# PEER's one-hot grids: which side of the matmul carries the weight, and a contiguous copy of the other side

## The chip, the cores and the metric

The kernel runs on one core of a Trainium2 chip. The metric is the device time of one execution in microseconds (us). Before the change it is 3071.65 us, the median of three runs (3069.44 to 3080.57).

## The reference

Two transformer blocks run one after the other on 512 tokens of width 1024. The change lies in the last layer of the second block, PEER: each token picks 128 of 16384 one-neuron experts (8 heads, 16 each), by two indices i and j of 128 each.

```python
def one_chunk(hb):
    q = (hb @ w_q).reshape(C, PEER_HEADS, 2, PEER_DK_HALF)
    s = jnp.einsum('thpd,hpnd->thpn', q, sub_keys)
    sv, si = lax.top_k(s, PEER_TOPK)
    ...
    fv, fpos = lax.top_k(cand, PEER_TOPK)
    eidx = jnp.take_along_axis(cidx, fpos, axis=-1).reshape(C, PEER_HEADS * PEER_TOPK)   # i * 128 + j
    g = jax.nn.softmax(fv, axis=-1).reshape(C, PEER_HEADS * PEER_TOPK)
    u = u_tab[eidx]
    a = jax.nn.gelu(jnp.einsum('ted,td->te', u, hb), approximate=False)
    coef = (g * a).astype(hb.dtype)
    return jnp.einsum('te,ted->td', coef, v_tab[eidx])
```

## The kernel before

The first 128 tokens take their rows of the tables `u` and `v` by gather (`own`, L1293): an indirect DMA on GpSimd (POOL) for each of 256 rows and one VectorE instruction on each (L1309 or L1313). The other 384 tokens are computed dense. For every j, `act` (L1267) loads a block of 128 experts, splits it into a high and a low part (`whi` by ScalarE L102, `wlo` by VectorE or POOL L103), multiplies it with all 384 tokens in 24 matmuls of 384 columns (L122 to L124) and writes the GELU (L1274). These products must then be multiplied by each token's gates, and for that each token gets a grid of 128 x 128 numbers, zero but at its 128 experts.

A grid is one small matrix product over the token's 128 picks. The picks lie on the 128 partitions. On one side stands a one-hot row of i for each pick, on the other a one-hot row of j times the pick's gate. The gate is held as two f16 parts (`WW[:, 0]` and `WW[:, 1]`), so a grid is two matmuls that add into the same place in PSUM, of 128 columns each, and both load the same stationary one-hot anew.

VectorE makes the one-hots for four tokens at a time (`onehots`, L1442; `OT` is 4), in a layout in which the token is the innermost index: element (i, token) of a tile lies at 4 i + token, so that the 128 values of one token are 8 bytes apart in f16. A set is four VectorE instructions: `oi` by comparing with i (L1450), `on` by comparing with j (L1452), and `on` times each of the two gate parts into `oj` (L1455, twice). `oi` and `oj` have three buffers (`OB`), `on` two.

`grids` (L1458) takes 128 tokens in 32 units of four tokens; a unit is eight matmuls (L1475, four tokens by two gate parts) into one PSUM bank, and a ScalarE instruction that moves the bank to the tile `G` (L1477). There are three such groups of tokens, so 96 units and 768 of these matmuls. Between the units the program sets other work: `unit` (L1497) adds .6508 expert blocks and .7 gathered rows to each unit of the first two groups, .7484 and .8 in the third; the picking of the next group of tokens (`picks`) runs in between. A scheduler turns this program into one order for each engine; each engine then works through its own order and waits where a semaphore is not up yet.

Of the kernel before, what the change touches and what calls it, by code (L numbers as in the profile page):

```python
# [11 lines left out]
F16 = mybir.dt.float16  # L12
# [4 lines left out]
OP = mybir.AluOpType  # L17
# [14 lines left out]
OT, OB, HL = 4, 3, 4  # L32
# [8 lines left out]
class Kern:  # L41
# [1198 lines left out]
    def peer(self):  # L1240
        nc, tc, I = self.nc, self.tc, self.I
        mm = nc.tensor.matmul
# [6 lines left out]
        with ExitStack() as cx:  # L1249
# [7 lines left out]
            IT, JT = [pi.tile([128, TD], F16, name=n) for n in ("IT", "JT")]  # L1257
            WW = pi.tile([128, 2, TD], F16, name="WW")
# [71 lines left out]
            for h in range(2):  # L1330
                bk = self.bank("x")
# [23 lines left out]
            with tc.tile_pool(name="pe2", bufs=2) as q2:  # L1355
# [4 lines left out]
                for hp in range(16):  # L1360
                    bk = bks[hp] if hp < 3 else self.feat_major(wq(hp), hT)
                    qT = q2.tile([128, T], F32, name="qT")
                    nc.scalar.copy(qT, bk)
                    bk = self.bank("x")
# [77 lines left out]
            def onehots(t, done):  # L1442
                sh = [128, OT // 4, 128, 4]
                of = lambda v: v.rearrange("p (g t) -> p g t", t=4)[:, :, None, :].to_broadcast(sh)
                io = io4[:, None].to_broadcast(sh)
                for tk in range(t * 128 - 128, t * 128, OT):
                    oi, on = [q4.tile(sh, F16, name=n, bufs=b) for n, b in (("oi", OB), ("on", 2))]
                    oj = q4.tile([128, 2] + sh[1:], F16, name="oj", bufs=OB)
                    done.append((oi, oj))
                    nc.vector.tensor_tensor(oi, io, of(IT[:, tk:tk + OT]), op=OP.is_equal)  # L1450
                    yield
                    nc.vector.tensor_tensor(on, io, of(JT[:, tk:tk + OT]), op=OP.is_equal)  # L1452
                    yield
                    for w in range(2):
                        nc.vector.tensor_mul(oj[:, w], on, of(WW[:, w, tk:tk + OT]))  # L1455
                        yield

            def grids(t):  # L1458

                gout = iter(())  # L1460
                hots = []
                hot = onehots(t, hots)
                for _ in range(HL):
                    next(hot)
                for c in range(128 // CT):
                    G = gp.tile([128, 128, CT], F32, name="G")
                    for u in range(0, CT, 4):
                        bk = self.bank("x")
                        for _ in range(16 // OT):
                            next(hot, None)  # L1470
                        if u % OT == 0:
                            oi, oj = hots.pop(0)
                        for e in range(4):
                            for w in range(2):
                                mm(bk[:, e * 128:(e + 1) * 128], oi[:, u % OT // 4, :, e], oj[:, w, u % OT // 4, :, e],  # L1475
                                   start=(w == 0), stop=(w == 1))
                        nc.scalar.activation(G[:, :, u:u + 4], bk.rearrange("p (t j) -> p j t", t=4), AF.Copy,  # L1477
                                             scale=1.0 / WSC)
                        if u % 8 == 4:
                            next(gout, None)  # L1480
                        yield
                    n = (t - 1) * (128 // CT) + c
                    gout = spill(n, G)
                    if n >= CD - KG:
                        last.append(G)
                        gout = iter(())
                for _ in gout:
                    pass

            def spill(c, G):  # L1490
                for k in range(0, 128, 2048 // CT // 2):
                    n = 2048 // CT // 2
                    nc.sync.dma_start(gd[c, 0:128, k * CT:(k + n) * CT], G[:, k:k + n].rearrange("p j t -> p (j t)"))
                    yield
# [19 lines left out]
            for t in range(NT):  # L1514
                if t == 0:
                    for _ in picks(t):
                        pace(FA, 0)
                    for u in range(1, NT):
                        for _ in tops(u):
                            pace(FT, S0)  # L1520
                    cs.close()
                    q4 = cy.enter_context(tc.tile_pool(name="pe3b", bufs=2))
                    gp = cx.enter_context(tc.tile_pool(name="pegg", bufs=2, side="right"))
                    prev = iter(())
                    continue
                for _ in picks(t):
                    pace(FB, S1)
                    unit(prev, 3)
                unit(prev, 128)
                late[0] = t - 1  # L1530
                prev = grids(t)
# [155 lines left out]
```

## Time and profile before

| | |
|---|---|
| time, median of three runs | 3071.65 us |
| time of the profiled execution | 3062.43 us |
| its span, first to last instruction | 3060.7 us |
| busy TensorE (PE), VectorE (DVE), ScalarE (ACT), POOL | 2933.6, 2093.2, 1156.9, 636.3 us |
| mean granted TensorE clock | 0.980 |
| the grids: first and last matmul of L1475 start at | 2000.2 and 2387.0 us |

The profile is of one execution. Times in it are counted from the first instruction. PE is the matmuls, PEld the loading of the stationary operand, which runs beside them. A matmul's record reaches to the end of its passage through the array, so that neighbours' records overlap: how fast matmuls follow each other is read from their starts, not from their durations. "Idle before, releaser" says what an engine waited for.

### The profile page before, as it was taken

How to read it: one execution, taken by the hardware profiler on the slowest of the kernel's cores; microseconds unless marked ns; L12 is line 12 of the kernel's file. 1: busy time of each engine (PE TensorE's matmuls, PEld its weight loads, DVE VectorE, ACT ScalarE, POOL GpSimd, SP SyncE). 2: the span in 40 equal slices, each digit the busy share in tenths (PEclk: the TensorE clock that was granted, in tenths of full speed). 3: DMA queues.
4: the chain of work that ended last, by engine and by line, in shares of the span. 5: the costliest groups of instructions: out<-in, count | busy, mean ns of one | idle time of the engine just before them, and what ended most of it. 6: DMA issues, size and time to landing. Idle time of an engine off the chain costs nothing.

```text
span 3060.7 us, 43629 instructions
## 1 busy us (share of the span) xinstructions
PE 2933.6 (96%) x16121; PEld 2473.6 (81%) x16121; DVE 2093.2 (68%) x4710; ACT 1156.9 (38%) x1918; POOL 636.3 (21%) x593
## 2 busy tenths in 40 slices
PE   7987998999999999999999999999999999999998
PEld 6765887888888788888865888889999888787887
DVE  7773767333255666425775778999988488787887
ACT  5634333322233322223565433343443333333332
POOL 1033220000000000000000004435444334444443
PEclk9988999999999999999999999999999999999999
DMA  4356553223343277432220225678888899999996
GB/s 141 96 144 184 148 146 127 91 96 96 90 131 103 83 237 231 138 95 89 85 70 8 88 96 192 223 251 305 288 292 284 276 327 336 315 329 324 323 329 228
DMA packets 217555, 569.04 MB, mean 186 GB/s; under 512 B 64475, under 2 KB 80091, under 8 KB 217213
## 3 DMA queue, kind: packets, MB, share of 16 engines
q1 hardware_dynamic: 144508, 362.71, 36.4%
q0 software_dynamic: 64096, 200.89, 19.4%
q10 hardware_dynamic: 8736, 2.65, 0.4%
q8 instruction: 126, 2.06, 0.3%
q14 instruction: 89, 0.72, 0.1%
HBM read 504.24 MB, written 61.87 MB: 185 GB/s over the span
## 4 chain that ended last, share of the span: by engine, by line
PE 74%; DVE 12%; DMA 7%; issue 4%; ACT 2%; POOL 1%; POOLq 0%; DVEq 0%; ACTq 0%; SPq 0%
PE b L276 18%; PE b L124 15%; PE b L123 15%; PE b L122 15%; DMA gl<-ga 3%; PE b L1475 3%; DVE wlo L103 2%; DVE hr L1313 1%; DVE er L1309 1%; PE b L1166 1%; DMA er<-in_pe_ur,eu 1%; PE b L964 1%; DVE wk L1344 1%; DMA sp_v<-vv 1%; PE b L1184 1%
## 5 line engine op out<-in xcount | busy, mean ns | idle before, releaser
L102 ACT CAST whi<-wst 128x1024 fp32r<-128x1024 f32 (+2 forms) x491 | 510.4, 1041 | 1162.1 <-PE b L123 483.3
L103 DVE TENSOR_TENSOR wlo<-wst,whi 128x1024 fp32r<-128x1024 f32 (+2 forms) x466 | 563.5, 1211 | 442.2 <-ACT whi L102 420.0
L124 PE MATMUL b<-hTh,wlo 128*128 128x384 f32 (+2 forms) x1992 | 718.0, 361 | 14.9 <-DVE wlo L103 14.7
L122 PE MATMUL b<-hTh,whi 128*128 128x384 f32 (+2 forms) x1992 | 723.3, 364 | 2.9 <-ACT hTh L223 1.9
L123 PE MATMUL b<-hTl,whi 128*128 128x384 f32 (+2 forms) x1992 | 718.2, 361 | 2.1 <-DVE hTl L224 2.1
L124 PEld LDWEIGHTS b<-hTh,wlo 128*128 128x128 f32 x1992 | 379.0, 190 | 58.2 <-DVE wlo L103 19.5
L122 PEld LDWEIGHTS b<-hTh,whi 128*128 128x128 f32 x1992 | 380.5, 191 | 42.8 <-ACT hTh L223 2.6
L123 PEld LDWEIGHTS b<-hTl,whi 128*128 128x128 f32 x1992 | 379.6, 191 | 40.9 <-DVE hTl L224 2.9
L122 PE MATMUL b<-whi,ch 128*128 128x512 f32 x768 | 304.9, 397 | 5.9 <-ACT ch L102 5.9
L123 PE MATMUL b<-wlo,ch 128*128 128x512 f32 x768 | 304.9, 397 | 2.4 <-DVE wlo L103 2.4
L124 PE MATMUL b<-whi,cl 128*128 128x512 f32 x768 | 304.9, 397 | 1.2 <-DVE cl L103 1.2
L1297 POOL DMA_INDIRECT er<-in_pe_v,ev x128 | 191.2, 1494 | 251.5 <-DVE hr L1313 227.5
L1297 POOL DMA_INDIRECT er<-in_pe_ur,eu x128 | 167.0, 1305 | 89.7 <-DVE er L1309 57.7
L122 PEld LDWEIGHTS b<-whi,ch 128*128 128x128 f32 x768 | 144.9, 189 | 40.4 <-ACT ch L102 6.2
L123 PEld LDWEIGHTS b<-wlo,ch 128*128 128x128 f32 x768 | 144.9, 189 | 37.8 <-DVE wlo L103 3.6
L124 PEld LDWEIGHTS b<-whi,cl 128*128 128x128 f32 x768 | 144.8, 189 | 36.7 <-DVE cl L103 1.9
L1313 DVE SCALAR_TENSOR_TENSOR hr<-er,a,hr 128x1024 f32<-128x1024 f32 x127 | 166.5, 1311 | 0.1
L1309 DVE SCALAR_TENSOR_TENSOR er<-er,hr 128x1024 f32<-128x1024 f32 x128 | 157.2, 1231 | 4.8 <-DMA er<-in_pe_ur,eu 4.7
L1279 POOL DMA_DIRECT2D ga<-gl x112 | 64.9, 579 | 347.6 <-ACT gl L1274 333.7
L276 PE MATMUL b<-whi,hTh 128*128 128x512 f32 (+2 forms) x336 | 129.3, 386 | 0.8 <-ACT P L976 0.8
L276 PE MATMUL b<-whi,hTl 128*128 128x512 f32 (+2 forms) x336 | 129.4, 385 | 0.4 <-DVE hTl L103 0.4
L276 PE MATMUL b<-wlo,hTh 128*128 128x512 f32 (+2 forms) x336 | 129.6, 386 | 0.0
(558 smaller groups left out, 4922.7 us busy)
## 6 DMA issues: line engine op xcount, KB each, us to landing
wst<-in_pe_u SPq DMA_DIRECT2D x128, 512.0 KB, 5.0
wst<-in_pe_v SPq DMA_DIRECT2D x128, 512.0 KB, 6.3
wst<-in_ffn_gu SPq DMA_DIRECT2D x88, 512.0 KB, 3.7
wst<-in_ad_w SPq DMA_DIRECT2D x48, 512.0 KB, 4.1
wst<-in_ffn_dn SPq DMA_DIRECT2D x44, 512.0 KB, 3.6
ga<-gl POOLq DMA_DIRECT2D x112, 192.0 KB, 4.2
gl<-ga SPq DMA_DIRECT2D x112, 192.0 KB, 5.4
gd<-G SPq DMA_DIRECT2D x40, 512.0 KB, 6.8
```

The lines of the kernel that those rows point to most:

```text
L102: self.nc.scalar.copy(hi, src)
L103: (eng or self.nc.vector).tensor_sub(lo, src, hi)
L122: mm(out, a[0], b[0], start=start, stop=False)
L123: mm(out, a[0], b[1], start=False, stop=False)
L124: mm(out, a[1], b[0], start=False, stop=stop)
L276: self.nc.tensor.matmul(banks[t][:, :n], self.chunk(aT, a, k + kk)[:, t * 128:(t + 1) * 128], w[b][:, kk, :], start=seen[t] == 1, stop=see ...
L964: self.nc.tensor.transpose(bk[:, c * 128:(c + 1) * 128], src[:, c * 128:(c + 1) * 128], self.ident)
L1279: nc.gpsimd.dma_start(ga[j], act(j))
L1297: d = nc.gpsimd.indirect_dma_start(out=r, out_offset=None, in_=src, in_offset=bass.IndirectOffsetOnAxis(ap=idx[:, k:k + 1], axis=0))
L1309: d = nc.vector.scalar_tensor_tensor(r, r, 1.0, hr, op0=OP.mult, op1=OP.mult, accum_out=a0[:, k:k + 1])
L1313: d = nc.vector.scalar_tensor_tensor(y0, r, a0[:, k - 128:k - 127], y0, op0=OP.mult, op1=OP.add)
L1475: mm(bk[:, e * 128:(e + 1) * 128], oi[:, u % OT // 4, :, e], oj[:, w, u % OT // 4, :, e], start=(w == 0), stop=(w == 1))
```

## The change

The two gate parts go to the i side, which stays in the interleaved layout and stays the stationary operand; `oi` now has the two parts and `os` is the plain one-hot from which they are made. The j side is a plain one-hot, `on`, made first; ScalarE copies it into `oj` with each token's 128 values side by side, and that copy is the moving operand. A set is still four VectorE instructions, and one ScalarE instruction more. `oj` shrinks to half, `oi` doubles, and `os` (two buffers) is new.

```diff
-                    oi, on = [q4.tile(sh, F16, name=n, bufs=b) for n, b in (("oi", OB), ("on", 2))]
-                    oj = q4.tile([128, 2] + sh[1:], F16, name="oj", bufs=OB)
+                    os, on = [q4.tile(sh, F16, name=n) for n in ("os", "on")]
+                    oi = q4.tile([128, 2] + sh[1:], F16, name="oi", bufs=OB)
+                    oj = q4.tile([128, OT, 128], F16, name="oj", bufs=OB)
                     done.append((oi, oj))
-                    nc.vector.tensor_tensor(oi, io, of(IT[:, tk:tk + OT]), op=OP.is_equal)
+                    nc.vector.tensor_tensor(on, io, of(JT[:, tk:tk + OT]), op=OP.is_equal)
+                    nc.scalar.copy(oj, on.rearrange("p g i t -> p (g t) i"))
                     yield
-                    nc.vector.tensor_tensor(on, io, of(JT[:, tk:tk + OT]), op=OP.is_equal)
+                    nc.vector.tensor_tensor(os, io, of(IT[:, tk:tk + OT]), op=OP.is_equal)
                     yield
                     for w in range(2):
-                        nc.vector.tensor_mul(oj[:, w], on, of(WW[:, w, tk:tk + OT]))
+                        nc.vector.tensor_mul(oi[:, w], os, of(WW[:, w, tk:tk + OT]))
                         yield
...
                             for w in range(2):
-                                mm(bk[:, e * 128:(e + 1) * 128], oi[:, u % OT // 4, :, e], oj[:, w, u % OT // 4, :, e],
+                                mm(bk[:, e * 128:(e + 1) * 128], oi[:, w, u % OT // 4, :, e], oj[:, u % OT + e],
                                    start=(w == 0), stop=(w == 1))
```

Line numbers of the changed kernel are two higher behind the function: the grids' matmul is L1477 there and the move to `G` is L1479; the copy is L1452, the two comparisons are L1451 (`on`) and L1454 (`os`), the products L1457. The order of the matmuls on TensorE is nearly the same: runs of 24 matmuls of an expert block and then one or two units of grids.

ScalarE in the third group of tokens, before; `G` is the grid tile, `whi` the high part of an expert block, `gl` its GELU, and what an instruction waits for stands in brackets:

```order
L1477 ACTIVATE G<-b_21342 128x128x4 [waits PE_49]
L1477 ACTIVATE G<-b_21359 128x128x4 [waits PE_49]
L102 CAST whi<-wst 128x1024 [waits DMAHW0_49,DVE_49,PE_49]
L1274 ACTIVATE gl<-b_21383 128x384 [waits DMASW1_49,PE_49]
L1477 ACTIVATE G<-b_21415 128x128x4 [waits DMAHW2_49,DMAHW4_49,DMAHW1_49,PE_49]
L102 CAST whi<-wst 128x1024 [waits DMAHW1_49,DVE_49,PE_49]
L1274 ACTIVATE gl<-b_21438 128x384 [waits DMASW3_49,PE_49]
```

and the same place now:

```order
L1479 ACTIVATE G<-b_21516 128x128x4 [waits PE_49]
L1479 ACTIVATE G<-b_21535 128x128x4 [waits PE_49]
L1452 COPY oj<-on 128x512 [waits DVE_49] x2
L102 CAST whi<-wst 128x1024 [waits DMAHW0_49,PE_49]
L1274 ACTIVATE gl<-b_21561 128x384 [waits DMASW1_49,PE_49]
L1479 ACTIVATE G<-b_21593 128x128x4 [waits DMAHW2_49,DMAHW4_49,DMAHW1_49,PE_49]
L1452 COPY oj<-on 128x512 [waits DVE_49]
L102 CAST whi<-wst 128x1024 [waits DMAHW1_49,PE_49]
L1274 ACTIVATE gl<-b_21618 128x384 [waits DMASW3_49,PE_49]
```

Behind each move to `G` there is now a copy, which waits for VectorE, and the next `whi` stands behind it.

VectorE in the third group of tokens, before; `wlo` is the low part of an expert block, `er` a gathered row:

```order
L1452 TENSOR_TENSOR on<-io_14630,JT 128x512 [waits DVE_49]
L1450 TENSOR_TENSOR oi<-io_14630,IT 128x512 [waits PE_49]
L1455 TENSOR_TENSOR oj<-on,WW 128x512 x2
L103 TENSOR_TENSOR wlo<-wst,whi 128x1024 [waits DMAHW6_49,Activation_49]
L1309 SCALAR_TENSOR_TENSOR er,a_14638<-er,hr 128x1024 [waits DMASW2_49]
```

and now:

```order
L1451 TENSOR_TENSOR on<-io_14630,JT 128x512 [waits Activation_49]
L1454 TENSOR_TENSOR os<-io_14630,IT 128x512 [waits DVE_49]
L1457 TENSOR_TENSOR oi<-os,WW 128x512 [waits PE_49]
L1457 TENSOR_TENSOR oi<-os,WW 128x512
L1457 TENSOR_TENSOR oi<-os,WW 128x512 [waits DVE_49,PE_49]
L1457 TENSOR_TENSOR oi<-os,WW 128x512
L1309 SCALAR_TENSOR_TENSOR er,a_14638<-er,hr 128x1024 [waits DMASW4_49]
```

The wait for TensorE has moved from the comparison to the first product, and the comparison that makes `on` now waits for ScalarE, which must have copied the `on` of two sets before.

## Rows read from the trace of the kernel before

**Rows 1.** The page's first part: busy us (share of the span) xinstructions.

```profile
PE 2933.6 (96%) x16121; PEld 2473.6 (81%) x16121; DVE 2093.2 (68%) x4710; ACT 1156.9 (38%) x1918; POOL 636.3 (21%) x593
```

**Rows 2.** Stretches of the grids and after: us, busy by engine, clock, DMA share, GB/s.

```profile
2000.00:2260.00 260.00, 257.99 (x1628) 248.86 (x1628) 244.92 (x505) 112.22 (x172) 119.51 (x104) 0.99 0.82 283
2260.00:2390.00 130.00, 130.00 (x825) 125.48 (x825) 102.01 (x192) 51.01 (x81) 62.42 (x57) 1.00 0.84 287
...
2430.00:2700.00 270.00, 264.81 (x1155) 217.89 (x1156) 213.34 (x394) 92.31 (x128) 105.46 (x82) 0.98 0.92 319
```

**Rows 3.** Waits of DVE, 2000 to 2260, then 2260 to 2390: us, times, longest.

```profile
DVE oi L1450 <- PE b L1475: 6.1, 10, 2.3
DVE wlo L103 <- ACT whi L102: 5.6, 2, 2.8
DVE er L1309 <- DMA er<-in_pe_ur,eu: 1.9, 1, 1.9
...
DVE oi L1450 <- PE b L1475: 18.8, 19, 2.2
DVE wlo L103 <- PE b L1475: 5.8, 1, 5.8
DVE wlo L103 <- ACT whi L102: 1.9, 1, 1.9
```

**Rows 4.** Timeline of PE around two runs of grid matmuls: start us, us, what.

```profile
2154.53 1.11 PE L1475 MATMUL b<-oj,oi 128*128 128x128 f16 x8
2155.40 0.42 PE L122 MATMUL b<-hTh,whi 128*128 128x384 f32 x1
2155.66 0.34 PE L123 MATMUL b<-hTl,whi 128*128 128x384 f32 x1
...
2164.93 2.06 PE L1475 MATMUL b<-oj,oi 128*128 128x128 f16 x16
2166.74 0.43 PE L122 MATMUL b<-hTh,whi 128*128 128x384 f32 x1
2167.01 0.33 PE L123 MATMUL b<-hTl,whi 128*128 128x384 f32 x1
```

**Rows 5.** Timeline of PE, matmuls of 256 columns that lie side by side.

```profile
1743.25 0.28 PE L123 MATMUL b<-hTl,whi 128*128 128x256 f32 x1
1743.36 0.28 PE L124 MATMUL b<-hTh,wlo 128*128 128x256 f32 x1
...
1744.88 0.28 PE L122 MATMUL b<-hTh,whi 128*128 128x256 f32 x1
```

**Rows 6.** PEld by line and shape: busy us, mean ns of one | idle before.

```profile
L122 PEld LDWEIGHTS b<-hTh,whi 128*128 128x128 f32 x1992 | 380.5, 191 | 42.8 <-ACT hTh L223 2.6 <-ACT whi L102 1.1 <-ACT hTh L102 0.4
L1475 PEld LDWEIGHTS <-oi 128*128 128x128 f16 x768 | 81.3, 118 | 21.5 <-issue 15.7 <-DVE oj L1455 2.7 <-DVE on L1452 1.1
...
L778 PEld LDWEIGHTS b<-wlo,M 128*64 128x64 f32 x256 | 24.1, 138 | 0.9 <-issue 0.5 <-POOL wlo L768 0.3
```

**Rows 7.** Timelines cut inside the run at 2164.93: its first loads, its first matmuls.

```profile
2164.92 0.15 PEld L1475 LDWEIGHTS <-oi 128*128 128x128 f16 x2 [0.16 <-issue]
...
2164.93 0.29 PE L1475 MATMUL b<-oj,oi 128*128 128x128 f16 x1
...
2164.93 0.41 PE L1475 MATMUL b<-oj,oi 128*128 128x128 f16 x2
...
2164.93 0.53 PE L1475 MATMUL b<-oj,oi 128*128 128x128 f16 x3
```

**Rows 8.** Timeline of PE: small matmuls in close order.

```profile
308.28 0.92 PE L754 MATMUL b<-Nd,Y 128*64 128x64 f32 x24 [0.37 <-ACT Y L746]
```

**Rows 9.** ACT by line, 2000 to 2390: busy us, mean ns of one | idle before.

```profile
L102 ACT CAST whi<-wst 128x1024 fp32r<-128x1024 f32 x70 | 73.8, 1054 | 199.9 <-PE b L123 166.9 <-issue 32.0 <-ACT whi L102 1.0
L1477 ACT ACTIVATE G<-b 128x512 f32<-128x512 f32 x96 | 56.6, 593 | 17.3 <-PE b L1475 15.4
L1274 ACT ACTIVATE gl<-b 128x384 f32<-128x384 f32 x70 | 33.9, 484 | 0.0
```

**Rows 10.** DVE by line, 2000 to 2390: the one-hot instructions.

```profile
L1455 DVE TENSOR_TENSOR oj<-on,WW 128x512 f16<-128x512 f16 x192 | 100.2, 563 | 0.0
...
L1450 DVE TENSOR_TENSOR oi<-io,IT 128x512 f16<-128x512 f16 x94 | 39.3, 420 | 25.1 <-PE b L1475 24.9
L1452 DVE TENSOR_TENSOR on<-io,JT 128x512 f16<-128x512 f16 x95 | 38.2, 417 | 0.0
```

## The prediction

> **What bounds the kernel now.** I began with the busy shares of the page [rows 1]: TensorE is busy 96% of the span, VectorE 68%, so time comes from TensorE, if at all. Then the same by stretches [rows 2], since the change touches only 2000 to 2390 us: there TensorE is busy 388 of 390 us, and VectorE is close behind, 244.9 of 260 us while two groups of grids run beside the picking of the next group, then 102.0 of 130 us. VectorE's waits [rows 3] say who leads: for 6.1 us of the first stretch and 18.8 us of the second it waits for a buffer that the grid matmuls still read. So TensorE decides the stage, with a margin over VectorE of 15.1 us in the first stretch and 28.0 us in the second. What TensorE saves counts in full only up to these margins.
>
> **What a grid matmul costs.** Two timelines give it by a difference that has the same edges on both sides [rows 4]: from the start of a run of 8 to the second matmul behind it is 2155.66 - 2154.53 = 1.13 us, from a run of 16 it is 2167.01 - 2164.93 = 2.08 us. Eight more cost 0.95 us, 119 ns each. The 768 cost 91 us.
>
> What are those 119 ns? Matmuls of 256 columns that lie side by side follow each other in 116 ns (14 steps from 1743.25 to 1744.88) [rows 5], so a grid matmul of 128 columns takes as long as one of 256: half rate. It might be the load of the stationary side instead. A load's record is 191 ns for 128 columns of f32 and 138 ns for 64 [rows 6]: 53 ns per 64 columns on top of some 85 ns that are the same for both. The grids' f16 load is 118 ns, which leaves 33 ns of loading. The run's start agrees [rows 7]: the first two loads are over after 0.15 us, so the second ends some 0.03 us after the first; yet the ends of the first three matmuls lie 0.12 us apart (0.29, 0.41, 0.53). The second matmul had its stationary side in time and still came 0.12 us later. So I take it that the moving side is streamed at half rate, and that its step of 8 bytes is the reason: it is what sets it apart from the matmuls of [rows 5].
>
> **The change part by part.**
>
> *Moving side contiguous.* 128 columns at the rate of [rows 5] are 58 ns. Small matmuls with a load each follow at under 0.92 / 24 = 38 ns [rows 8], so the issue of a pair doesn't stand in the way, and 33 ns of load fit beside 58. No row shows f16 columns side by side: the bounds are 119 ns (the step is not the reason, nothing saved) and 58 ns. I take 60 ns, near the lower end, because of [rows 7]. Saved: 59 ns x 768 = 45 us of TensorE, 30 us of it in the first stretch (512 matmuls), 15 us in the second (256).
>
> The Trainium skill has a measured pace for this: TensorE: Matmul & The Clock Gate, section "Back-to-back issue gap", gives about 81 ns for each pair of load and matmul at 128 columns in a real kernel. No row here has such a pair. By it 38 ns x 768 = 29 us would be saved, 19 and 10 us in the two stretches.
>
> *Stationary side with two parts.* Still 768 loads, with the same 8-byte step: 118 ns each as before, beside the matmuls. Nothing.
>
> *VectorE.* Two comparisons and two products a set before and after, of the same size and layout [rows 10]: nothing, in work. The wait for a free buffer moves from the first instruction to the third, which is better by up to 0.8 us a set where VectorE waits for TensorE.
>
> *The copy on ScalarE.* 96 copies of 512 elements. There is no such row; the nearest are 593 ns for 512 elements out of PSUM in a scattered order, 484 ns for 384, 1054 ns for 1024 in order [rows 9]. I take 0.6 us (0.5 if the f16 source helps, 1.2 if the step of 8 bytes halves it): 58 us. ScalarE is busy 163 of 390 us [rows 2], so 221 with it. The copies stand in front of the next `whi`, and before that cast ScalarE has idled 166.9 us over 70 casts for TensorE to release its buffer [rows 9], 2.4 us each; one or two copies (0.6 to 1.2 us) fit into that. Cost nothing there; without that cover it would be 58 us on ScalarE's chain, and the expert blocks would come late.
>
> *The new wait.* `on` waits for the copy two sets back. Behind it VectorE holds the products that TensorE wants, and `wlo`. That copy stands behind the move to `G` of a unit some four sets back, which is earlier than the matmuls for which the first product waits anyway. Where all is on time it costs nothing; with 0.05 us of handshake on some 60 of the 96 sets I take 3 us, bounds 0 and 1.2 us (a move and a copy) on every set.
>
> *What ends last then.* In the first stretch TensorE would need 260 - 30 = 230 us, VectorE 244.9: VectorE takes over. Of its 15.1 us of waits the 6.1 us for TensorE go, and about half of the 5.6 us for a `whi` that itself waits for TensorE [rows 3]: 9 us gained. In the second stretch TensorE needs 115 us, VectorE 102: all 15 us are gained. 9 + 15 - 3 = 21 us. The stage becomes 6% shorter, so the DMA rate must rise from 287 to about 303 GB/s; later the kernel moves 319 [rows 2]. What follows the grids shifts forward as it is.
>
> The profiled execution took 3062.4 us (span 3060.7), and becomes 3041. The median of the runs is 9.2 us above it; I take the 21 us off that: 3051 us.
>
> **The rivals.**
>
> *The step costs nothing.* Then the 119 ns are something in the f16 load or its order, and stay. For it: the load's record, 118 ns [rows 6], is within 1 ns of the pace, as if each pair waited for its load, and no matmul here differs from the grids in the step alone. Against it: [rows 7]. TensorE saves nothing, VectorE and ScalarE stay covered: 0 to +4 us, 3072 us.
>
> The Trainium skill speaks for this one: SBUF — State Buffer, section "Specifications (TRN2)", says that memory lines have 16 bytes and that two hits in a line are enough for full bandwidth. A step of 8 bytes has just two. By that rule the moving side ran at full rate before; [rows 4] do not look like it, but do not exclude it.
>
> *The handshake decides (slower).* VectorE has 15.1 us of slack in the first stretch for 64 sets, so a wait of 0.24 us a set at `on` is the point from which it, and not TensorE, makes the stage longer. If ScalarE is held at a `whi` while a copy stands behind it, the wait is about one copy, 0.6 us: 64 x 0.6 - 15 = +23 us; in the second stretch 32 x 0.6 = 19 us against 28 - 15 = 13 us of slack, +6 us against the 15 us gained. 3072 + 23 + 6 - 15 = 3086 us. For it: the waits in the new order. Against it: the copy needed lies two sets back.
>
> *VectorE is no bound.* Its products average 563 ns where the comparisons take 417 to 420 [rows 10]; 192 x 0.14 = 28 us that the work itself, the same 512 elements, does not explain. If these go when TensorE runs ahead, the first stretch gains its 30 us too, and all 45 us come through: 3027 us.
>
> **How the numbers follow.** Forecast (pace 58 to 85 ns, VectorE takes over in the first stretch) 0.60, own range 3040 to 3062; step costs nothing 0.20; handshake 0.10; no bound by VectorE 0.10. About 0.5% (15 us) is what a measurement of this kernel can tell from no change: 3056 to 3087. Faster: 0.47 of the forecast's 0.60 and the last rival, 0.57. Slower: the worse part of the handshake and 0.02 of the second, 0.08. Same 0.35. The range 3032 to 3076 us leaves out the better part of the last rival (0.07), the handshake from its middle on (0.08) and a little of the first rival.
>
> **What would show it.** Right: eight more grid matmuls cost about 0.48 us; copies near 0.6 us; TensorE now waits for `oi` between 2000 and 2250, and not after; the grids end about 21 us sooner. Wrong: a pace still near 119 ns (the step was not it); VectorE idle at `on` L1451 for ScalarE by more than 15 us; `whi` late, so that TensorE waits in expert blocks; or a stage that gets shorter by 40 us.

## The result and the profile after

| | before | after |
|---|---|---|
| median (lowest to highest), 4 runs each | 3076.11 us (3069.44 to 3087.63) | 3046.45 us (3018.76 to 3054.05) |
| profiled execution, its span | 3062.43, 3060.7 us | 3054.05, 3051.4 us |
| first and last grid matmul | 2000.2, 2387.0 us | 2004.9, 2365.9 us |

The ratio is 0.9896, with a 95% interval of 0.9858 to 0.9935: about 1% faster. The profiled execution after is the slowest of its four, so its span shows less than the median does; the stage itself can be read in it all the same.

The page's first part, after, answers to [rows 1]:

```profile
PE 2906.6 (95%) x16121; PEld 2440.9 (80%) x16121; DVE 2090.9 (69%) x4710; ACT 1209.1 (40%) x2014; POOL 647.3 (21%) x593
```

TensorE is busy for 27 us less in this execution and ScalarE for 52 us more, in 96 instructions more; VectorE's work is the same. The three groups of 128 tokens, each from its first grid matmul to the next group's, first before and then after (columns as in [rows 2]: us, then busy of PE, PEld, DVE, ACT and POOL, clock, DMA share, GB/s):

```profile
2000.20:2131.30 131.10, 129.32 (x812) 124.29 (x811) 125.47 (x270) 55.37 (x85) 58.53 (x51) 0.99 0.79 277
2131.30:2263.10 131.80, 131.77 (x832) 127.40 (x832) 121.49 (x240) 58.21 (x89) 61.57 (x54) 1.00 0.84 289
2263.10:2387.00 123.90, 123.90 (x791) 119.65 (x791) 99.20 (x188) 48.88 (x77) 59.44 (x54) 1.00 0.83 286
```

```profile
2004.90:2132.80 127.90, 117.95 (x811) 113.08 (x812) 125.49 (x270) 72.41 (x118) 66.88 (x51) 0.95 0.82 291
2132.80:2256.40 123.60, 121.08 (x831) 116.24 (x832) 121.81 (x246) 75.53 (x122) 65.64 (x54) 0.97 0.85 296
2256.40:2365.90 109.50, 109.50 (x793) 105.95 (x792) 93.39 (x181) 64.20 (x106) 60.42 (x53) 1.00 0.91 324
```

In the third group TensorE was busy all the time and still is: its 14.4 us come through whole. In the first two VectorE has the same 247 us of work, and the groups have shrunk from 262.9 to 251.5 us, close to that. TensorE is now the one that waits, 10 us of it in the first group. Together the grids take 361.0 us instead of 386.8: 25.8 us.

Waits of PE from 1995 to 2400, first before and then after, then those of DVE after, from 2005 to 2256 and from 2256 to 2370 (us, times, longest), for [rows 3]:

```profile
PE b L1475 <- DVE oj L1455: 8.7, 2, 6.9
```

```profile
PE b L1477 <- DVE oi L1457: 17.2, 4, 7.1
PE b L124 <- DVE wlo L103: 2.0, 1, 2.0
```

```profile
DVE on L1451 <- ACT oj L1452: 1.9, 2, 1.2
...
DVE oi L1457 <- PE b L1477: 2.3, 3, 1.0
DVE on L1451 <- ACT oj L1452: 0.6, 1, 0.6
```

VectorE waits for TensorE for 2.3 us instead of 24.9, and none of it in the first two groups. For the copy it waits 2.5 us in all. Of TensorE's waits, 6.9 us before and 6.8 us after lie ahead of the first grid matmul, and so outside the groups. The longest wait of TensorE stands at the change from the first group to the second, where VectorE has the picking of tokens on its hands:

```profile
2132.80 0.30 PE L1477 MATMUL b<-oj,oi 128*128 128x128 f16 x1 [7.14 <-DVE oi L1457]
2132.86 0.67 PE L122 MATMUL b<-hTh,whi 128*128 128x384 f32 x1
2133.33 0.97 PE L1477 MATMUL b<-oj,oi 128*128 128x128 f16 x7
```

The matmul of 384 columns behind it lasts 0.67 us where 0.34 is usual: the granted clock has fallen during the wait. The stretch ahead of it, with it and behind it, in the columns of the table above:

```profile
2120.00:2125.00 5.00, 5.00 (x32) 4.97 (x31) 5.00 (x16) 1.49 (x4) 0.61 (x1) 1.00 0.97 333
2125.00:2135.00 10.00, 2.86 (x16) 2.20 (x14) 10.00 (x30) 2.17 (x5) 1.62 (x2) 0.79 0.99 395
2135.00:2145.00 10.00, 10.00 (x67) 9.37 (x66) 9.89 (x20) 7.24 (x12) 6.21 (x5) 0.87 0.47 155
```

TensorE is back at work, and for part of those ten microseconds at 1.2 instead of 2.4 GHz (0.87). The 0.95 and 0.97 of the first two groups are such places.

A run of 8 and a run of 16 grid matmuls after, for [rows 4], and the loads, for [rows 6]:

```profile
2155.63 0.64 PE L1477 MATMUL b<-oj,oi 128*128 128x128 f16 x8
2156.08 0.42 PE L122 MATMUL b<-hTh,whi 128*128 128x384 f32 x1
2156.34 0.34 PE L123 MATMUL b<-hTl,whi 128*128 128x384 f32 x1
...
2165.10 1.09 PE L1477 MATMUL b<-oj,oi 128*128 128x128 f16 x16
2165.99 0.42 PE L122 MATMUL b<-hTh,whi 128*128 128x384 f32 x1
2166.25 0.34 PE L123 MATMUL b<-hTl,whi 128*128 128x384 f32 x1
```

```profile
L1477 PEld LDWEIGHTS <-oi 128*128 128x128 f16 x768 | 47.6, 117 | 30.3 <-issue 12.3 <-DVE oi L1457 12.2 <-PE b L123 1.1
```

From the start of a run to the second matmul behind it: 1.15 us for 16, 0.71 for 8, so eight more cost 0.44 us. Over all runs of the stage the medians are 1153 and 706 ns, so a matmul costs 55.9 ns (before 2076 and 1129 ns, 118.4). With its edges a run of 8 became 0.42 us shorter and one of 16 0.92 us, on all 768 some 42 us. A load's record is still 117 ns; it never was the pace.

ScalarE and VectorE by line, 2000 to 2370, for [rows 9, 10] (busy us, mean ns of one, idle before):

```profile
L102 ACT CAST whi<-wst 128x1024 fp32r<-128x1024 f32 x70 | 73.7, 1057 | 107.6 <-PE b L123 51.0 <-DMA wst<-in_pe_u 30.9 <-issue 21.1
L1452 ACT COPY oj<-on 128x512 f16<-128x512 f16 x96 | 61.9, 667 | 26.4 <-DVE on L1451 26.3
```

```profile
L1457 DVE TENSOR_TENSOR oi<-os,WW 128x512 f16<-128x512 f16 x192 | 79.9, 462 | 2.4 <-PE b L1477 2.3
...
L1454 DVE TENSOR_TENSOR os<-io,IT 128x512 f16<-128x512 f16 x96 | 44.5, 468 | 0.0
L1451 DVE TENSOR_TENSOR on<-io,JT 128x512 f16<-128x512 f16 x96 | 44.1, 462 | 2.6 <-ACT oj L1452 2.5
```

The copies have taken the place of ScalarE's waiting: in front of `whi` 51 us of waiting for TensorE are left of 167. The products have become quicker and the comparisons slower, which nothing in the change explains; the last two experiments do.

### The profile page after: what moved, and what is told of

Same layout as the page of the kernel before. It is cut to its first block, busy times and chain, and to the rows that moved or that the text cites. A ratio compares the mean times of both kernels' runs of the same rounds, so it can differ in the third digit from the quotient of the medians.

```text
span 3051.4 us, 43847 instructions
## 1 busy us (share of the span) xinstructions
PE 2906.6 (95%) x16121; PEld 2440.9 (80%) x16121; DVE 2090.9 (69%) x4710; ACT 1209.1 (40%) x2014; POOL 647.3 (21%) x593
## 4 chain that ended last, share of the span: by engine, by line
PE 66%; DVE 15%; DMA 9%; issue 5%; ACT 3%; POOL 1%; POOLq 0%; DVEq 0%; ACTq 0%; SPq 0%
PE b L276 19%; PE b L123 12%; PE b L124 12%; PE b L122 12%; DMA gl<-ga 4%; DVE wlo L103 3%; DVE er L1309 2%; DVE hr L1313 1%; DMA wst<-in_pe_v 1%; PE b L1477 1%; PE b L1166 1%; PE b L964 1%; DMA er<-in_pe_ur,eu 1%; PE b L1184 1%; DVE cl L103 1%
## 5 line engine op out<-in xcount | busy, mean ns | idle before, releaser
L1297 POOL DMA_INDIRECT er<-in_pe_ur,eu x128 | 177.8, 1389 | 90.8 <-DVE er L1309 59.6
L123 PEld LDWEIGHTS b<-wlo,ch 128*128 128x128 f32 x768 | 145.8, 190 | 46.9 <-DVE wlo L103 12.5
```

The source lines that it names most:

```text
L123: mm(out, a[0], b[1], start=False, stop=False)
L1297: d = nc.gpsimd.indirect_dma_start(out=r, out_offset=None, in_=src, in_offset=bass.IndirectOffsetOnAxis(ap=idx[:, k:k + 1], axis=0))
```

## The experiments

Milestones are read from each run's trace: the start of the first grid matmul, of the 257th, the 513th and the last.

**The changed kernel again.** Of the 25.8 us gained in the grids the profiled execution kept only 9.3: it started them 4.7 us late and was 12.5 us longer in the v matmuls behind them (2408.8 to 3041.9, against 2430.6 to 3051.2). Is that a price of the change?

> The changed kernel again, for a second profile and a closer interval. In the first profile the grids ended 21 us sooner than before (2365.9 against 2387.0 us), yet the span was only 9 us shorter, and the four times lay between 3019 and 3054 us. Theory A: the 21 us at the grids are steady, and the last stretch, where expert blocks of v come in at a DMA share of 0.93, takes sometimes 10 to 15 us more or less by itself: the grids end at 2366 +- 4 us again, the time is 15 to 35 us under before (ratio 0.988 to 0.995). Theory B: the earlier end of the grids costs some 12 us in the last stretch each time (its DMAs collide with more): the last stretch, from its first matmul to the end, is again longer by 10 us or more than the 620.6 us of before.

Measured: 3046.13 us against 3072.92, ratio 0.9922 (0.9895 to 0.9948). Grids 128.2 + 122.7 + 109.1 = 360.0 us, the v matmuls 620.7 us as before (620.6), span 3039.0, 21.7 less than before. So the tail of 633.1 us does not come with the change each time. Whether a smaller price does is open: in the traces of all the kernels below that keep the quick matmuls the v matmuls take 617.3 to 631.4 us, in those with the slow ones 619.6 to 624.5. The medians, 26.8 and 29.7 us apart in the two comparisons, leave it little room. The late start (2003.7) is set ahead of the change's code: L1334, some 280 us earlier, was late already (1727.1 in the first profile against 1721.9 us before), and in the traces of kernels that are the same up to there it starts anywhere from 1714.8 to 1730.3 us.

**The copy stays, the step of 8 bytes too.**

```diff
-                    oj = q4.tile([128, OT, 128], F16, name="oj", bufs=OB)
+                    oj = q4.tile(sh, F16, name="oj", bufs=OB)
-                    nc.scalar.copy(oj, on.rearrange("p g i t -> p (g t) i"))
+                    nc.scalar.copy(oj, on)
-                               oj[:, u % OT + e],
+                               oj[:, u % OT // 4, :, e],
```

> The changed kernel, but ScalarE's copy leaves the layout as it is: the moving operand has its 8-byte step again; the copy, its waits and all orders stay. Theory step: the pace of grid matmuls goes back from 56 to 118 or 119 ns, the grids end at 2385 us or later and the time is within 5 us of before or above it (ratio 0.998 to 1.006). Theory order (the pace fell because another operand is weighted, or because of buffers and orders): the pace stays at 56 ns and the time is that of the changed kernel, some 25 us under before.

Measured: 3072.78 us, ratio 1.0001 (0.9979 to 1.0024); grids 389.4 us. A run of 8 in its trace:

```profile
2152.37 1.11 PE L1477 MATMUL b<-oj,oi 128*128 128x128 f16 x8
2153.24 0.42 PE L122 MATMUL b<-hTh,whi 128*128 128x384 f32 x1
2153.50 0.34 PE L123 MATMUL b<-hTl,whi 128*128 128x384 f32 x1
```

1.13 us to the second matmul behind, to the hundredth what it was before [rows 4]. The gain hangs on the step of the moving operand; who carries the weight gives nothing, to within 0.2%.

**Steps of 4 and of 12 bytes.** Two theories say what the pace hangs on: a contiguous operand as against any other, or the bytes from a row's first value to its last. In the first kernel two tokens share a tile, in the second six values stand where four are used.

```diff
 # 4 bytes
+                    oj = q4.tile([128, OT // 2, 128, 2], F16, name="oj", bufs=OB)
+                    nc.scalar.copy(oj, on.rearrange("p g i (a b) -> p (g a) i b", b=2))
+                               oj[:, (u % OT + e) // 2, :, (u % OT + e) % 2],
 # 12 bytes
+                    oj = q4.tile([128, OT // 4, 128, 6], F16, name="oj", bufs=OB)
+                    nc.scalar.copy(oj[:, :, :, 0:4], on)
+                               oj[:, u % OT // 4, :, e],
```

> The changed kernel, but the copy sets two tokens side by side, so that the moving operand steps by 4 bytes. Theory span (the moving side is read at a fixed number of bytes a cycle, gaps included, and 4 bytes a column is what the f32 operands need too): the pace stays at 56 to 60 ns. Theory contiguous (only values side by side go at full rate): the pace is near 118 ns.

> The changed kernel, but the copy sets the values of a token 12 bytes apart. Theory span: three times the bytes of a 4-byte step, a pace near 3 x 57 = 170 to 180 ns. Theory half rate (a step beyond some size halves the rate, whatever it is): near 118 ns. TensorE then needs some 430 us for the grids by the first theory, about 390 by the second.

Measured, one run each: 3047.97 and 3110.05 us; grids 360.1 and 427.1 us. A run of 8 with 4 bytes, then runs of 16 and of 8 with 12:

```profile
2153.98 0.66 PE L1477 MATMUL b<-oj,oi 128*128 128x128 f16 x8
2154.44 0.42 PE L122 MATMUL b<-hTh,whi 128*128 128x384 f32 x1
2154.70 0.34 PE L123 MATMUL b<-hTl,whi 128*128 128x384 f32 x1
```

```profile
2155.25 2.96 PE L1477 MATMUL b<-oj,oi 128*128 128x128 f16 x16
2157.91 0.48 PE L122 MATMUL b<-hTh,whi 128*128 128x384 f32 x1
2158.22 0.34 PE L123 MATMUL b<-hTl,whi 128*128 128x384 f32 x1
...
2162.21 1.56 PE L1477 MATMUL b<-oj,oi 128*128 128x128 f16 x8
2163.47 0.49 PE L122 MATMUL b<-hTh,whi 128*128 128x384 f32 x1
2163.79 0.33 PE L123 MATMUL b<-hTl,whi 128*128 128x384 f32 x1
```

With 4 bytes it is 0.72 us, as when contiguous (0.71). With 12 bytes eight more cost 2.97 - 1.58 = 1.39 us. Over all runs: 55.9 ns at 2 bytes, 59.6 at 4, 118.4 at 8, 174 at 12. Up to 4 bytes the step is nearly free; from there the cost grows with the span, 58 to 60 ns for each 4 bytes of step at 128 columns, gaps included. The theories by which only contiguous values go fast, or any wide step halves the rate, fall.

**The copy alone.** The kernel before, with a copy that nothing reads.

```diff
                     nc.vector.tensor_tensor(on, io, of(JT[:, tk:tk + OT]), op=OP.is_equal)
+                    cj = q4.tile([128, OT, 128], F16, name="cj", bufs=OB)
+                    nc.scalar.copy(cj, on.rearrange("p g i t -> p (g t) i"))
```

> The kernel before, with ScalarE's copy of the j one-hot into a tile of its own that nobody reads: the price of the copy and of VectorE's wait for it, with the matmuls as before. Theory cover: the copies (0.66 us each) lie in ScalarE's idle time and the wait at the j one-hot is rarely felt: the grids last 387 +- 4 us, ratio 0.998 to 1.003. Theory handshake: each set costs 0.1 to 0.2 us on VectorE, the grids last 395 us or more, ratio 1.003 or above.

Measured: 3073.83 us against 3068.15, ratio 1.0022 (1.0003 to 1.0041). The copies cost 61 us of ScalarE (663 ns each), and the grids took 387.7 us, as before. By the interval the copies cost the whole kernel 1 to 13 us; the profiled grids show none of it.

**The copy twice.** After the change, with a second copy of the same size into a tile that nothing reads.

```diff
                     nc.scalar.copy(oj, on.rearrange("p g i t -> p (g t) i"))
+                    cj = q4.tile([128, OT, 128], F16, name="cj", bufs=1)
+                    nc.scalar.copy(cj, on.rearrange("p g i t -> p (g t) i"))
```

> The changed kernel with a second copy of the same tile on ScalarE that nobody reads (64 us more on ScalarE, some 285 us of the grids' 361). Theory cover: ScalarE still has room before its casts: the grids last 361 +- 5 us and the time is within 6 us of the changed kernel. Theory ScalarE: the casts of expert blocks come late, TensorE waits for wlo or whi in expert blocks and the grids last 370 us or more.

Measured: 3052.01 us, ratio 0.9932 (0.9906 to 0.9959); grids 362.6 us. VectorE's waits for ScalarE, 1995 to 2395, and a wait of TensorE, 1995 to 2400:

```profile
DVE wlo L103 <- ACT whi L102: 20.0, 10, 7.1
...
DVE on L1451 <- ACT oj L1452: 3.6, 5, 1.0
DVE on L1451 <- ACT cj L1454: 2.1, 3, 0.9
```

```profile
PE b L1479 <- ACT oj L1452: 4.7, 2, 3.2
```

The waits for `whi` lie almost all outside the grids (after the change they are 26.8 us in the same window). Another 64 us on ScalarE cost the stage 2 us: the cover is real. It is close to used up, for TensorE now waits 4.7 us for the copy itself, and never did after the change.

**One product instead of two.** VectorE's work is cut, to see whether it holds the first two groups. The second part of the gate is left out of the result.

```diff
-                        nc.vector.tensor_mul(oi[:, w], os, of(WW[:, w, tk:tk + OT]))
+                        if w == 0:
+                            nc.vector.tensor_mul(oi[:, w], os, of(WW[:, w, tk:tk + OT]))
-                               oi[:, w, u % OT // 4, :, e],
+                               oi[:, 0, u % OT // 4, :, e],
```

> The changed kernel without the product for the second gate part: VectorE has 96 instructions fewer (0.42 to 0.56 us each, 40 to 54 us), the second matmul reads the first part once more, so TensorE and ScalarE have the same work; the grids then hold twice the first part. Theory VectorE: in the first two groups VectorE decides; they shorten from 251.5 to about 230 us (TensorE's own need), the third group stays at 109 us, the time falls by 15 to 22 us under the changed kernel (ratio to before 0.983 to 0.989). Theory handshake: what TensorE waits for there is the copy on ScalarE and its place in the order; then the first two groups stay within 5 us of 251 us and the time with them.

Measured: 3042.12 us, ratio 0.9907 (0.9872 to 0.9942). The first two groups, in the columns of the group table:

```profile
2010.30:2135.50 125.20, 117.33 (x811) 113.27 (x811) 123.08 (x269) 78.77 (x123) 65.66 (x51) 0.95 0.81 285
2135.50:2254.40 118.90, 118.90 (x834) 115.26 (x835) 100.84 (x181) 68.66 (x117) 65.82 (x54) 0.98 0.90 325
```

They fell by 7 us, less than the 15 to 22 expected. In the second group VectorE has 21 us less to do and TensorE no idle time: there VectorE had held the stage, and when it is 4.7 us shorter TensorE holds it. In the first group VectorE is as full as ever, with as many instructions: other work has moved up into the place of the products. TensorE's waits for `oi`, 14.7 us in three pieces, are the ones at the picking, and stay: 6.8 us ahead of the grids, 3.4 and 4.5 us in the first group.

**Fewer gathered rows, or more expert blocks, in the first two groups.** If VectorE is the bound there and TensorE in the third, work can be shifted between them: rows of the gather (VectorE's) to the third group, or expert blocks (TensorE's) to the first two.

```diff
 # rows later
-S0, S1, S2, SL, S3 = .3, .2, .7, .8, 1.2492
+S0, S1, S2, SL, S3 = .3, .2, .55, 1.1, 1.2492
 # blocks earlier, and more of it
-FA, FT, FB, FG, FL = .2, .5, .2, .6508, .7484
+FA, FT, FB, FG, FL = .2, .5, .2, .7, .65
+FA, FT, FB, FG, FL = .2, .5, .2, .74, .57
```

> The changed kernel with the gathered rows that VectorE works on beside the grids set otherwise: .55 instead of .7 a unit in the first two groups, 1.1 instead of .8 in the third; their number up to the end of the grids is the same (54.4 and 54.4), 9.6 rows move. Theory VectorE: 9.6 rows at 1.3 us are 12 us less in the first two groups, where VectorE decides (251 to about 240 us), and 12 us more in the third, where it is busy for some 80 of 109 us and has room: the time is 6 to 12 us under the changed kernel. Theory handshake or DMA: nothing gained in the first two groups, or the third becomes longer by as much as they gain: time within 4 us of the changed kernel.

> The changed kernel with .70 instead of .6508 expert blocks a unit in the first two groups of tokens and .65 instead of .7484 in the third: some 3.1 blocks move from the third group, where TensorE is the bound (109.5 us, VectorE busy 92 of them), to the first two, where VectorE is (busy 248 of 251.5 us). Theory VectorE: the third group loses 3.1 x 4.2 = 13 us and ends at about 96, the first two gain some 3 us (the low parts of 3.1 blocks, 1.2 us each), so the grids last about 351 us and the time is 7 to 12 us under the changed kernel. Rival: the first two groups wait for something that more matmuls delay too (the casts, the DMA of blocks); they lengthen by 10 us or more and nothing is gained.

> As the run with .70 and .65, with .74 and .57: some 5.7 blocks move. TensorE's own need in the third group would be 109.5 - 24 = 85 us, under VectorE's 92, so VectorE decides there too: third group about 93 us, first two 251.5 + 6 = 257 us, the grids 350 us: by the theory VectorE no better than .70 and .65 (within 4 us). If TensorE were the bound in the first two groups, they would lengthen by 24 us and the grids would last as long as in the changed kernel or longer.

Measured:

| | groups, us | grids | time, us | ratio to before |
|---|---|---|---|---|
| change, again | 128.2 + 122.7 + 109.1 | 360.0 | 3046.13 | 0.9922 (0.9895 to 0.9948) |
| rows later | 126.8 + 118.8 + 119.0 | 364.6 | 3048.21 | 0.9920 (0.9892 to 0.9949) |
| blocks earlier | 133.7 + 122.4 + 97.2 | 353.3 | 3043.30 | 0.9907 (0.9887 to 0.9927) |
| more of it | 140.8 + 131.0 + 97.1 | 368.8 | 3051.76 | 0.9944 (0.9929 to 0.9959) |

Rows moved to the third group made it 10 us longer, which undid the 6 us gained in the first two: a miss. (By the settings 70.4 rows are due up to the end of the grids in both kernels, not 54.4.) VectorE did have room there, busy for 106.2 of 119.0 us, but the rows came late; its only waits from 2252.5 to 2371.5, and TensorE's:

```profile
DVE er L1309 <- DMA er<-in_pe_ur,eu: 12.7, 7, 3.4
```

```profile
PE b L124 <- DVE wlo L103: 6.0, 3, 3.5
```

At the longest of these VectorE stood at a row that had not landed, the `wlo` behind it came late, and TensorE waited for that; then it ran at 1.2 GHz for 6.8 us of the group. Blocks moved to the first two shorten the grids by 7 us; by the intervals that is not to be told from the change itself. More of it overshoots, another miss: the second group is then TensorE's again, busy for 130.88 of its 131.0 us, the first two groups are 20 us longer, near the 24 expected with TensorE as their bound, and the third gets no shorter. The room that VectorE's lead leaves to TensorE is no more than the 12.5 us that TensorE idles in the first two groups after the change.

**All low parts on VectorE, after and before.** Single one-hot instructions last 414 to 418 ns in the median, before and after; the means of 563 and 462 ns come from 12 and 8 instructions of 1.9 to 3.3 us. One of them before, and POOL at the same time:

```profile
2160.88 0.43 DVE L1450 TENSOR_TENSOR oi<-io,IT 128x512 f16<-128x512 f16 x1 [0.20 <-PE b L1475]
2161.22 2.97 DVE L1455 TENSOR_TENSOR oj<-on,WW 128x512 f16<-128x512 f16 x2
```

```profile
2160.94 2.64 POOL L103 TENSOR_TENSOR wlo<-wst,whi 128x1024 fp32r<-128x1024 f32 x1 [2.03 <-PE b L1475]
```

The first of the two products alone lasts 2.64 us, to 0.28 us behind the end of POOL's `wlo` (2163.58). All 20 of the long ones end so. Sixteen began after POOL's `wlo`; four began 0.6 us ahead of it, while POOL was issuing a gather's DMA. Every fifth expert block has its `wlo` made by POOL; both kernels were run with none.

```diff
-WP = 5
+WP = 1000
```

> The changed kernel with every low part `wlo` of the expert blocks on VectorE; POOL makes none (before: 14 or 15 of 71 in the grids). Theory A: a one-hot instruction that runs while POOL makes a `wlo` is held until POOL is done, 2.2 us too long; that is all of the surplus over 415 ns (18.3 us in 8 instructions after the change). Then no one-hot instruction lasts over 600 ns, all three kinds average about 415 ns; VectorE gets 15 x 1.22 = 18 us of new work for about 18 us of holds and some held `er`, so the grids stay within 4 us of 361 and the time within 8 us of the changed kernel's 3046. Theory B: the long ones wait for TensorE's use of the buffers: 8 or more of them remain over 600 ns, and the grids grow by the 18 us of new work, to about 375 us, time 3060.

> The kernel before with every `wlo` on VectorE. Theory A: the products' mean falls from 563 to about 415 ns (28 us of holds in 12 instructions go, 14 x 1.22 = 17 us of work come), with TensorE at the old pace of 119 ns still the bound; grids within 4 us of 387 us, time within 8 us of the kernel before. Theory B: the mean stays above 520 ns, and VectorE with 17 us more work takes the lead in the first two groups: grids about 390 to 400 us.

Measured: no one-hot instruction over 600 ns is left in either. The products, 1995 to 2395, after and before:

```profile
L1457 DVE TENSOR_TENSOR oi<-os,WW 128x512 f16<-128x512 f16 x186 | 70.4, 420 | 3.5 <-PE b L1477 3.5
```

```profile
L1455 DVE TENSOR_TENSOR oj<-on,WW 128x512 f16<-128x512 f16 x191 | 72.6, 418 | 0.0
```

The grids took 364.6 and 390.8 us, 4 us more than with POOL's help, though the 1.22 us that a `wlo` takes on VectorE stand for the 2.2 us that a held one-hot lost; what the 4 us are was not followed up. So far theory A. The times, 3035.86 and 3059.70 us, ratios 0.9895 (0.9844 to 0.9945) and 0.9974 (0.9950 to 0.9999), were to lie within 8 us of their kernels and look some 10 us lower, a miss; the first interval overlaps that of the change. The traces put part of it ahead of the grids: from L1334 to the first grid matmul they take 272.7 and 271.2 us, all other traces 277.6 to 281.1. Four VectorE instructions of that stretch, some 6 us too long in all before, have no counterpart here; whether they are the reason was not tried. No version was shown to be faster than the change itself.

## Why the prediction was right, step by step

*TensorE bounds the stage, VectorE is next.* Shown. In the third group the length is TensorE's busy time before and after, and in the first two the waits have changed sides.

*The step of 8 bytes is the reason for the pace, and not the load.* Shown, by putting the step back under the new code. 60 ns were forecast and 55.9 came. By whole runs, edges included, some 42 us of TensorE were saved instead of 45; the third group's 14.4 us, a third of the matmuls, agree. The rival by which the step costs nothing fell. The Trainium skill, SBUF — State Buffer, section "Specifications (TRN2)", asks for two hits or more in a line of 16 bytes for full bandwidth. A step of 8 bytes has two and runs here at 118.4 ns, one of 4 bytes at 59.6, so for TensorE's moving side the measurement decides against reading it as enough. The Trainium skill, TensorE: Matmul & The Clock Gate, section "Back-to-back issue gap", gives some 81 ns for a pair of load and matmul at 128 columns. In the runs of 8 and 16 here a pair costs 55.9 ns, so 81 ns are no floor.

*The copy is covered.* 0.6 us were taken and 0.67 measured. Shown twice for the grids: with the copy alone they stayed as they were, and with a second one they grew by 2 us.

*The handshake costs 3 us.* 2.5 us of waiting for the copy were in the trace. The rival that made it decide would have shown 38 us of it in the first stretch alone.

*In the first stretch VectorE takes over, 9 us gained; in the second all 15.* 11.4 and 14.4 us came, the wait for the copy already in them; the forecast took 3 us off the two together for that wait. What the step left out is how VectorE's lead shows: not as a slower pace all along, but as a stop where the picking stands in front of the next group's one-hots, with 10 us of idle TensorE in the first group and a lower clock behind each stop. That is where the rest of the 42 us went, by an estimate from the traces: 25.8 us came through, TensorE's idle time in the groups rose from 1.8 to 12.5 us, and it worked 18 us at 1.2 GHz instead of 4, which costs half of the difference, 7 us. With a quarter less one-hot work only 7 us more came.

*The sum.* 21 us off 3062 in the profile, 25.8 measured in the grids and 21.7 off the span in the second execution; 3051 us as the median, 3046 measured. That the median came within 5 us is partly luck, for the four runs lie between 3018.76 and 3054.05. The offset between the profile and the runs was the coarser part: the shown profile moved by only 8.4 us, for reasons outside the grids.

*The last rival* held that the products' 28 us over the comparisons would go when TensorE runs ahead. They had nothing to do with TensorE: they are gone when POOL makes no `wlo`. The Trainium skill has it in SBUF — State Buffer, section "Who interferes with whom": a VectorE instruction with two inputs in SBUF and a POOL instruction that reads SBUF share one read interface, and the later waits for the earlier to end. The traces agree in 16 of the 20, 2.64 us where 0.415 is usual; in the other four the record of the VectorE instruction begins first. Read against the mean of 563 ns, that rule would have taken the rival its ground. It is luck of position which instructions are caught: one-hots lost 28 us before and 18 after, but with the gathered rows and one instruction of the picking VectorE lost 30 and 27 us, so that little was gained there.

## What to carry to other kernels

Lay the moving operand of a matmul so that its values lie at most 4 bytes apart: at 8 the f16 matmul took twice as long and at 12 three times, while the stationary side could stay interleaved at 8. A contiguous copy on an engine that idles in the same stage pays for that, if it stands where the engine waits anyway. What the bounding engine saves counts until another engine leads: of 42 us 26 came through here, and part of the rest went into stops and the lower clock behind them. And before a mean duration becomes a term or a rival, look at its median: a few instructions held by another engine look like a slow operation.

## What the runs showed of the hardware that was not expected

- The pace of f16 matmuls of 128 columns by the step of the moving operand: 2 bytes 55.9 ns, 4 bytes 59.6, 8 bytes 118.4, 12 bytes 174. From 4 to 12 bytes the time is in proportion to the span, with the unused bytes counted (512 bytes in 59.6 ns, 1536 in 174); wider steps were not run.
- A load of 128 f16 columns at a step of 8 bytes keeps out of the way of a pace of 56 ns, though its record reads 117 ns.
- A VectorE one-hot of 415 ns can be held by a `wlo` on POOL and end with it, up to 3.3 us after it began; all 20 long ones in the two traces lie so, and none is left when POOL makes no `wlo`. One-hots that VectorE had begun up to 0.4 us ahead of POOL's `wlo` kept theirs.
- A stop of 7 us costs more than 7 us: the granted clock was still 0.87 in the ten microseconds behind it, and single matmuls there took 0.67 us instead of 0.34.
